# Memory rows transposed before their norm is known, and the first weights asked for earlier, in a hybrid streaming encoder step

## The chip, the cores and the metric

The kernel runs on one core of a Trainium2 chip. Its time is the device time of one execution in microseconds (us). The median of three runs is the number that is compared.

## The reference

One inference step of a one-layer trunk, all in float32: 1024 prompt frames and 8 x 16 sample frames of width 1024, with stick-breaking attention, a Mamba-2 group and forgetting attention side by side, a cross-attention into 256 memory rows, a SwiGLU feed-forward part and a final norm. The part that matters here is the projection of the memory rows to keys and values, which is written out as an output as well:

```python
def rmsnorm(x, g):
    xf = x.astype(jnp.float32)
    y = xf * lax.rsqrt(jnp.mean(xf * xf, axis=-1, keepdims=True) + EPS)
    return (y * g.astype(jnp.float32)).astype(x.dtype)

def mem_kv(mem, g, wk, wv):              # mem (1, 256, 1024), wk and wv (1024, 1024)
    b, m, _ = mem.shape
    mn = rmsnorm(mem, g)
    k = jnp.einsum('bmd,de->bme', mn, wk).reshape(b, m, X_HEADS, X_HEAD_DIM)
    v = jnp.einsum('bmd,de->bme', mn, wv).reshape(b, m, X_HEADS, X_HEAD_DIM)
    return k, v
```

## The kernel before

All dense products are made of three float32r matmuls: each operand is split into a rounded high part and the remainder, and `mm3` adds high x high, high x low and low x high into one PSUM bank. A weight tile is loaded raw, cast on ScalarE (the high part, line 290) and subtracted on GpSimd in pieces of 256 columns (the low part, line 132, in `pool_tt`).

The kernel begins with constants and small loads (lines 138 to 224): the memory rows `xm` (two tiles of 128 x 1024), five vectors of gains and conv_b and the 32 rows of conv_w as rows of one tile `rows`, two raw weight tiles. One transpose of 72 rows turns `rows` into the columns `cols`; `g_mem` is a slice of them.

Then `mem_proj` runs (lines 812 to 836). `norm_T` squares the memory rows on ScalarE, takes the root with `rstd_of` (GpSimd and VectorE), scales the rows on VectorE, and then transposes them block by block on TensorE; the transposed blocks leave PSUM with the gain as a scale, the high part on ScalarE (line 276), the low part on VectorE (line 277). The projection itself is 16 units, each a weight tile of 256 x 512 (two k blocks) against both tiles of memory rows: 12 matmuls of 512 columns. Four units fill a pair of PSUM banks, which ScalarE copies out (line 833) and SyncE stores twice. At unit n the raw tile of unit n + 2 is asked for and split. The raw tiles are of the pool `st`, eight buffers.

After each unit one step of `aux` is emitted: the norm and the transposition of the prompt's rows in three chunks of 384 (`norm_in`, also by `norm_T`), whose squares write into a tile of the same pool `st`. The projections of the prompt, attention and the rest follow.

The program's text gives priority and data dependences; the order in each engine's queue is written by a planner that runs the program on simulated times (`schedule_with_timeline_sim=True`). All loads and stores go through SyncE's queue, in order.

Of the kernel before, what the change touches and what calls it, by code (L numbers as in the profile page):

```python
# [8 lines left out]
F32 = mybir.dt.float32  # L9
F32R = mybir.dt.float32r  # L10
I32 = mybir.dt.int32
AF = mybir.ActivationFunctionType
ALU = mybir.AluOpType
# [4 lines left out]
P = 128  # L18
D = 1024
KT = D // P  # L20
# [37 lines left out]
def f32(x):  # L58
    return x.bitcast(F32)
# [3 lines left out]
def tile_hybrid_step(ctx: ExitStack, tc: tile.TileContext, a: dict):  # L63
    nc = tc.nc
    ACT, DVE, POOL, PE, SP = nc.scalar, nc.vector, nc.gpsimd, nc.tensor, nc.sync
# [6 lines left out]
    mcst = left.enter_context(tc.tile_pool(name="mcst", bufs=1))  # L72
# [13 lines left out]
    def act_t(dt=F32R, home=None):  # L86
        return (home or actp).tile([P, 3072], dt, tag="act", name="act")
# [4 lines left out]
    def st_t(dt=F32R):  # L92
        return stp.tile([P, 1024], dt, tag="st", name="st")

    def ws_t(dt=F32):
        return wsp.tile([P, T], dt, tag="ws", name="ws")

    def xc_t(dt=F32):
        return xcp.tile([P, 1056], dt, tag="xc", name="xc")

    def sg_t(dt=F32):
        return sgp.tile([P, 512], dt, tag="sg", name="sg")
# [4 lines left out]
    def ps_t(pool, tag):  # L107
        return pool.tile([P, 512], F32, tag=tag, name="ps" + tag)
# [7 lines left out]
    def pT():  # L116
        return ps_t(pst, "t")
# [11 lines left out]
    def pool_tt(out, in0, in1, op):  # L129

        for a0, a1 in pieces_of(out.shape[1]):
            POOL.tensor_tensor(out=out[:, a0:a1], in0=in0[:, a0:a1], in1=in1[:, a0:a1], op=op)  # L132

    def small(n, dt=F32):
        return sm.tile([P, 16], dt, tag="sm", name="sm")[:, :n]


    xm = act_t(F32)
    for i in range(2):
        SP.dma_start(out=xm[:, i * D:(i + 1) * D], in_=a["mem_prompt"][0, i * P:(i + 1) * P, :])  # L140
    rows = xc_t()
    for i, g in enumerate(("norm_mix_g", "norm_x_g", "norm_ffn_g", "mem_norm_g", "conv_b")):
        SP.dma_start(out=rows[8 * i:8 * i + 8, :P], in_=a[g][0].rearrange("(k p) -> k p", p=P))
    SP.dma_start(out=rows[40:72, :P], in_=a["conv_w"][0].rearrange("i (k p) -> (i k) p", p=P))
    first_raw = []
    for k0 in (0, 2):
        first_raw.append(st_t(F32))
        SP.dma_start(out=first_raw[-1].rearrange("p (k n) -> p k n", n=512),
                     in_=a["wk_x"][0][k0 * P:(k0 + 2) * P, 0:512].rearrange("(k p) n -> p k n", p=P))


    ident = cst.tile([P, P], F32, name="ident")
# [2 lines left out]
    DVE.tensor_copy(identr, ident)  # L155
    mhalf = cst.tile([P, 1], F32, name="mhalf")
    POOL.memset(mhalf, -0.5)

    mask_sb = mcst.tile([P, P], F32R, name="mask_sb")
    mask_fx = mcst.tile([P, P], F32R, name="mask_fx")  # L160
# [55 lines left out]


    colp = pT()
    PE.transpose(colp[:, :72], rows[:72, :P], ident[:72, :72])
    cols = cst.tile([P, 72], F32, name="cols")  # L220
    DVE.tensor_copy(cols, colp[:, :72])
    DVE.tensor_scalar(cols[:, 32:72], cols[:, 32:72], 0.5, None, ALU.mult)
    g_mix, g_x, g_ffn, g_mem = (cols[:, 8 * i:8 * i + 8] for i in range(4))
    conv_b = cols[:, 32:40]

    hb = mcst.tile([P, 28], F32, name="hb")
    lf = mcst.tile([P, NBLK, 4], F32, name="lf")
    dts = mcst.tile([P, NBLK, 8], F32, name="dts")

# [19 lines left out]
    def rstd_of(ss, n, inv):  # L249
        v, r, t, r2 = small(n), small(n), small(n), small(n)  # L250
        POOL.tensor_scalar(v, ss, inv, EPS, ALU.mult, ALU.add)  # L251
        POOL.tensor_tensor(out=r, in0=v, in1=mhalf.to_broadcast([P, n]), op=ALU.pow)
        DVE.scalar_tensor_tensor(t, r, -0.5, r, ALU.mult, ALU.mult)
        DVE.tensor_tensor(out=t, in0=t, in1=v, op=ALU.mult)
        DVE.scalar_tensor_tensor(r2, t, 1.5, r, ALU.add, ALU.mult)
        return r2

    def norm_T(xs, g, hl, width, inplace=None):


        n = len(xs)
        xn = xs if inplace is not None else [ws_t() for _ in range(n)]
        ss = small(n)
        for i in range(n):
            ACT.activation(inplace if inplace is not None else xn[i][:, :D], xs[i], AF.Square,
                           accum_out=ss[:, i:i + 1])
        r = rstd_of(ss, n, 1.0 / D)
        for i in range(n):
            DVE.tensor_scalar(xn[i][:, :D], xs[i], r[:, i:i + 1], None, ALU.mult)
        yield  # L270
        hi, lo = hl()
        for k in range(KT):
            ps = pT()
            for i in range(n):
                PE.transpose(ps[:, i * P:(i + 1) * P], xn[i][:, k * P:(k + 1) * P], ident)
            ACT.activation(hi[:, k, :], ps[:, :width], AF.Copy, scale=g[:, k:k + 1])
            DVE.scalar_tensor_tensor(lo[:, k, :], ps[:, :width], g[:, k:k + 1], f32(hi[:, k, :]),
                                     ALU.mult, ALU.subtract)
            yield
# [6 lines left out]
    def unit_pair():  # L286
        return [ring.tile([P, 1056], F32R, tag=t, name=t) for t in ("wh", "wl")]

    def split_into(hi, lo, raw, eng=POOL):
        ACT.copy(hi, raw)  # L290
        if eng is POOL:
            pool_tt(lo, raw, f32(hi), ALU.subtract)
        else:
            eng.tensor_tensor(out=lo, in0=raw, in1=f32(hi), op=ALU.subtract)

    def split_unit(raw, n):
        hi, lo = unit_pair()
        split_into(hi[:, :n], lo[:, :n], raw[:, :n])
        return hi, lo

    def raw_t():

        return ring.tile([P, 528], F32, tag="wr", name="wr", bufs=4)

    def w_unit(srcs, k0, nk, raw=None, pair=None, eng=POOL):

        n = sum(s[2] for s in srcs)
        raws = [raw_t(), raw_t()] if raw is None else [raw]
        nk_ = nk // len(raws)
        for i, r in enumerate(raws):  # L310
            rv = r[:, :nk_ * n].rearrange("p (k n) -> p k n", n=n)
            o = 0
            for w, c0, cn in srcs:
                r0 = (k0 + i * nk_) * P
                SP.dma_start(out=rv[:, :, o:o + cn],
                             in_=w[r0:r0 + nk_ * P, c0:c0 + cn].rearrange("(k p) n -> p k n", p=P))
                o += cn
        hi, lo = pair or unit_pair()
        for i, r in enumerate(raws):
            sl = slice(i * nk_ * n, (i + 1) * nk_ * n)  # L320
            split_into(hi[:, sl], lo[:, sl], r[:, :nk_ * n], eng)
        return (hi[:, :nk * n].rearrange("p (k n) -> p k n", n=n),
                lo[:, :nk * n].rearrange("p (k n) -> p k n", n=n))
# [94 lines left out]
    def drain(g):  # L418
        for _ in g:
            pass  # L420
# [391 lines left out]
    def mem_proj(xm, aux):  # L812

        mh, ml = act_pair(256)
        drain(norm_T([xm[:, i * D:(i + 1) * D] for i in range(2)], g_mem, lambda: (mh, ml), 256, xm[:, 2 * D:]))
        work = [(a[wname][0], j, k0, sc, out) for wname, sc, out in (("wk_x", mk_sc, "p_mem_k"), ("wv_x", mv_sc, "p_mem_v"))
                for j in range(2) for k0 in (0, 2, 4, 6)]
        nxt = [[t[:, :1024].rearrange("p (k n) -> p k n", n=512) for t in split_unit(raw, 1024)] for raw in first_raw]
        for n, (w, j, k0, sc, out) in enumerate(work):
            wh, wl = nxt.pop(0)  # L820
            if n + 2 < len(work) :
                w2, j2, k2 = work[n + 2][:3]
                nxt.append(w_unit([(w2, j2 * 512, 512)], k2, 2, st_t(F32)))
            if k0 == 0:
                ps = [(pd, pS)[j % 2]() for _ in range(2)]
            for i in range(2):
                for k in range(2):
                    sl = slice(i * P, (i + 1) * P)
                    mm3(ps[i], mh[:, k0 + k, sl], ml[:, k0 + k, sl], wh[:, k, :], wl[:, k, :],
                        k0 + k == 0, k0 + k == KT - 1)  # L830
                if k0 == 6:
                    t = sg_t()
                    ACT.copy(t, ps[i])
                    for dst in (sc, a[out][0, 0].rearrange("m h d -> m (h d)")):
                        SP.dma_start(out=dst[i * P:(i + 1) * P, j * 512:(j + 1) * 512], in_=t)
            next(aux, None)


# [1065 lines left out]
    for kt in range(2, NFT):  # L1904
        nxt, ahead = left_factors(kt + 1, POOL) if kt + 1 < NFT else iter(()), []
# [57 lines left out]
    for c in range(NCH):  # L1963
# [3 lines left out]
        for f in range(NFT):  # L1967
            raw, hid = raw2_t(), slot()[:, :CW]
# [58 lines left out]
```

## Time and profile before

| | |
|---|---|
| median of three runs | 1915.68 us (1913.57 to 1916.64) |
| the profiled execution's own time | 1915.89 us |
| its span, first to last instruction | 1914.2 us |
| TensorE busy | 1837.6 us, 96% of the span |
| VectorE, ScalarE, GpSimd busy | 897.1, 823.7, 622.6 us |
| granted TensorE clock, mean | 0.988 |

The span is what the trace shows of the execution; 1.7 us lie around it. A busy TensorE is one with a matmul under way, whether at the upper or at the lower level of its clock.

### The profile page before, as it was taken

To read this page: it belongs to the slowest core of one execution; us is meant where nothing else is said; L and a number is where in the kernel's file an instruction comes from. 1 tells how busy PE (TensorE), PEld (TensorE's weight loads), DVE (VectorE), ACT (ScalarE), POOL (GpSimd) and SP (SyncE) were. 2 spreads that over 40 slices of the span, in tenths; PEclk is the share of its full clock that TensorE was granted. 3 is DMA by queue.
4 is the path that set the end of the run, shared out by engine and by line. 5 is a ranking of instruction groups with operands and counts; after the bars stand their busy time and mean duration, and the time that the engine had idled before them with its cause. 6 is when DMAs were issued, how large, how long until landed. Compare 5 with 4: busy or idle time off the path is not lost. (4 is left out here: it accounts for less than half of the span.)

```text
span 1914.2 us, 32508 instructions
## 1 busy us (share of the span) xinstructions
PE 1837.6 (96%) x12146; PEld 1641.4 (86%) x12146; DVE 897.1 (47%) x1823; ACT 823.7 (43%) x1782; POOL 622.6 (33%) x921
## 2 busy tenths in 40 slices
PE   7989989999998889999999999999999999999998
PEld 5889877888876667898998889999999999888886
DVE  3421323457646873353445387333333433455554
ACT  6431534545566771243433275333333333344443
POOL 7532416254324563211102205544444443000000
PEclk9999998999999999999999999999999999999999
DMA  9455645536579887244558124322323223567572
GB/s 336 142 165 159 211 115 152 154 109 185 166 220 282 280 290 260 103 150 145 176 194 291 66 91 111 80 70 70 95 74 75 70 70 100 190 194 237 177 246 92
DMA packets 309742, 305.70 MB, mean 160 GB/s; under 512 B 89996, under 2 KB 261108, under 8 KB 309584
## 3 DMA queue, kind: packets, MB, share of 16 engines
q1 hardware_dynamic: 309584, 303.62, 51.6%
q8 instruction: 96, 1.57, 0.3%
q14 instruction: 62, 0.51, 0.1%
HBM read 229.31 MB, written 74.24 MB: 159 GB/s over the span
## 5 line engine op out<-in xcount | busy, mean ns | idle before, releaser
L132 POOL TENSOR_TENSOR wl<-wr,wh 128x256 fp32r<-128x256 f32 (+2 forms) x184 | 138.6, 787 | 222.4 <-ACT wh L290 202.0
L326 PE MATMUL psd<-act,wh 128*128 128x384 f32 x576 | 198.7, 345 | 5.1 <-DVE sg L453 2.7
L327 PE MATMUL psd<-act,wh 128*128 128x384 f32 x576 | 197.6, 343 | 0.0
L328 PE MATMUL psd<-act,wl 128*128 128x384 f32 x576 | 196.8, 342 | 0.7 <-POOL wl L132 0.7
L1849 PE MATMUL pst<-bT,tr 128*128 128x256 f32 (+1 forms) x1068 | 155.0, 293 | 0.0
L1849 PEld LDWEIGHTS pst<-bT,tr 128*128 128x128 f32 x1068 | 144.9, 188 | 0.1
L328 PE MATMUL psd<-wh,act 128*128 128x512 f32 (+3 forms) x424 | 135.8, 322 | 0.0
L326 PE MATMUL psd<-wh,act 128*128 128x256 f32 (+3 forms) x414 | 133.0, 324 | 2.4 <-ACT pt L1445 1.2
L1849 PE MATMUL psd<-bT,tr 128*128 128x320 f32 (+1 forms) x912 | 133.2, 295 | 0.8 <-DVE tr L1693 0.5
L327 PE MATMUL psd<-wl,act 128*128 128x256 f32 (+3 forms) x414 | 132.8, 322 | 0.5 <-POOL wl L132 0.5
L1849 PEld LDWEIGHTS psd<-bT,tr 128*128 128x128 f32 x912 | 124.7, 188 | 1.8 <-DVE tr L1693 0.7
L326 PEld LDWEIGHTS psd<-act,wh 128*128 128x128 f32 x576 | 109.1, 189 | 8.7 <-DVE sg L453 3.1
L132 POOL TENSOR_TENSOR tr<-u,tr 128x256 fp32r<-128x256 f32 x110 | 81.9, 774 | 102.3 <-ACT tr L1689 85.1
L328 PEld LDWEIGHTS psd<-act,wl 128*128 128x128 f32 x576 | 108.9, 189 | 2.3 <-POOL wl L132 1.0
L327 PEld LDWEIGHTS psd<-act,wh 128*128 128x128 f32 x576 | 109.0, 189 | 1.5 <-issue 1.1
L132 POOL TENSOR_TENSOR ws<-ws 128x256 f32<-128x256 f32 (+2 forms) x100 | 68.5, 713 | 115.3 <-DVE ws L519 99.9
L1824 DVE TENSOR_TENSOR tr<-tr,pst 128x256 f32<-128x256 f32 (+1 forms) x86 | 38.6, 449 | 139.5 <-ACT tr L1821 106.3
L251 POOL TENSOR_SCALAR sm<-sm 128x1 f32<-128x1 f32 (+2 forms) x27 | 7.1, 261 | 296.6 <-ACT y L1932 208.0
L132 POOL TENSOR_TENSOR tr<-raw,tr 128x256 fp32r<-128x256 f32 x94 | 69.2, 765 | 84.5 <-ACT tr L1689 76.3
L1689 ACT CAST tr<-tr 128x384 fp32r<-128x384 f32 (+1 forms) x70 | 37.7, 538 | 121.1 <-DMA tr<-hidsc 104.3
L290 ACT CAST wh<-wr 128x512 fp32r<-128x512 f32 (+2 forms) x90 | 52.2, 621 | 80.7 <-PE psd L328 31.0
L326 PEld LDWEIGHTS psd<-wh,act 128*128 128x128 f32 x414 | 78.3, 189 | 9.9 <-ACT pt L1445 1.5
(620 smaller groups left out, 4714.0 us busy)
## 6 DMA issues: line engine op xcount, KB each, us to landing
u<-w_down SPq DMA_DIRECT2D x40, 512.0 KB
raw<-w_down SPq DMA_DIRECT2D x26, 512.0 KB
st<-qksc SPq DMA_DIRECT2D x48, 256.0 KB
wr<-w_in SPq DMA_DIRECT2D x44, 256.0 KB
tr<-hidsc SPq DMA_DIRECT2D x57, 192.0 KB
hidsc<-tr SPq DMA_DIRECT2D x34, 288.0 KB
qksc<-sg SPq DMA_DIRECT2D x48, 192.0 KB
wr<-cache_sb_k SPq DMA_DIRECT2D x32, 256.0 KB
```

The source lines that it names most:

```text
L132: POOL.tensor_tensor(out=out[:, a0:a1], in0=in0[:, a0:a1], in1=in1[:, a0:a1], op=op)
L251: POOL.tensor_scalar(v, ss, inv, EPS, ALU.mult, ALU.add)
L290: ACT.copy(hi, raw)
L326: PE.matmul(out, ah, bh, start=start, stop=False)
L327: PE.matmul(out, ah, bl, start=False, stop=False)
L328: PE.matmul(out, al, bh, start=False, stop=stop)
L1689: ACT.copy(hi, src)
L1824: DVE.tensor_tensor(out=at(out, g), in0=at(x, g), in1=ps[g][:, :GW[g]], op=op)
L1849: PE.matmul(dst[g][:, :GW[g]], x[:, ka], y[:, k, :], start=start and k == 0 and m == 0, stop=stop and k == 3 and m == 2, skip_group_check= ...
```

## The change

Four edits, all in the first part of the program.

The memory rows are transposed as they were loaded. Their squares and the root (`root`) are emitted after the first unit, and the root is applied to the finished products, as the scale of the copy out of PSUM.

The loads are put in another order: the first memory tile, the five small vectors, the second memory tile, four raw weight tiles instead of two, then conv_w. In `mem_proj` the raw tile is asked for four units ahead and split two units ahead. The low part of units 0, 1, 2, 5, 8, 11 and 14 is subtracted on VectorE in one instruction of 1024 columns, that of the others on GpSimd as before.

conv_w's rows have a transpose of their own (`tap_columns`), emitted after the second unit; the first transpose has 40 rows instead of 72.

A copy of one column on ScalarE stands ahead of all its other work, so that its function table is asked for there.

```diff
-    xm = act_t(F32)
-    for i in range(2):
+    xm, rows = act_t(F32), xc_t()
+    first_raw = []
+
+    def load_xm(i):
         SP.dma_start(out=xm[:, i * D:(i + 1) * D], in_=a["mem_prompt"][0, i * P:(i + 1) * P, :])
-    rows = xc_t()
+
+    def load_wk(n):
+
+        first_raw.append(st_t(F32))
+        SP.dma_start(out=first_raw[-1].rearrange("p (k n) -> p k n", n=512),
+                     in_=a["wk_x"][0][2 * n * P:(2 * n + 2) * P, 0:512].rearrange("(k p) n -> p k n", p=P))
+
+    load_xm(0)
     for i, g in enumerate(("norm_mix_g", "norm_x_g", "norm_ffn_g", "mem_norm_g", "conv_b")):
         SP.dma_start(out=rows[8 * i:8 * i + 8, :P], in_=a[g][0].rearrange("(k p) -> k p", p=P))
-    SP.dma_start(out=rows[40:72, :P], in_=a["conv_w"][0].rearrange("i (k p) -> (i k) p", p=P))
-    first_raw = []
-    for k0 in (0, 2):
-        first_raw.append(st_t(F32))
-        SP.dma_start(out=first_raw[-1].rearrange("p (k n) -> p k n", n=512),
-                     in_=a["wk_x"][0][k0 * P:(k0 + 2) * P, 0:512].rearrange("(k p) n -> p k n", p=P))
+    load_xm(1)
+    for n in range(4):
+        load_wk(n)
+    SP.dma_start(out=rows[64:96, :P], in_=a["conv_w"][0].rearrange("i (k p) -> (i k) p", p=P))
...
+    ACT.activation(small(1), mhalf, AF.Copy, scale=1.0)
...
-    PE.transpose(colp[:, :72], rows[:72, :P], ident[:72, :72])
+    PE.transpose(colp[:, :40], rows[:40, :P], ident[:40, :40])
     cols = cst.tile([P, 72], F32, name="cols")
-    DVE.tensor_copy(cols, colp[:, :72])
-    DVE.tensor_scalar(cols[:, 32:72], cols[:, 32:72], 0.5, None, ALU.mult)
+    DVE.tensor_copy(cols[:, 0:40], colp[:, :40])
+
+    def tap_columns():
+        tp = pT()
+        PE.transpose(tp[:, :32], rows[64:96, :P], ident[64:96, 64:96])
+        DVE.tensor_copy(cols[:, 40:72], tp[:, :32])
+        DVE.tensor_scalar(cols[:, 32:72], cols[:, 32:72], 0.5, None, ALU.mult)
...
-    def split_unit(raw, n):
+    def split_unit(raw, n, eng=POOL):
         hi, lo = unit_pair()
-        split_into(hi[:, :n], lo[:, :n], raw[:, :n])
+        split_into(hi[:, :n], lo[:, :n], raw[:, :n], eng)
         return hi, lo
...
-        drain(norm_T([xm[:, i * D:(i + 1) * D] for i in range(2)], g_mem, lambda: (mh, ml), 256, xm[:, 2 * D:]))
...
-        nxt = [[t[:, :1024].rearrange("p (k n) -> p k n", n=512) for t in split_unit(raw, 1024)] for raw in first_raw]
+
+        def unit(n):
+
+            return [t[:, :1024].rearrange("p (k n) -> p k n", n=512)
+                    for t in split_unit(first_raw.pop(0), 1024, DVE if n < 2 or n % 3 == 2 else POOL)]
+        nxt = [unit(0)]
+
+        for k in range(KT):
+            tp = pT()
+            for i in range(2):
+                PE.transpose(tp[:, i * P:(i + 1) * P], xm[:, i * D + k * P:i * D + (k + 1) * P], ident)
+            ACT.activation(mh[:, k, :], tp[:, :256], AF.Copy, scale=g_mem[:, k:k + 1])
+            DVE.scalar_tensor_tensor(ml[:, k, :], tp[:, :256], g_mem[:, k:k + 1], f32(mh[:, k, :]), ALU.mult, ALU.subtract)
+        nxt.append(unit(1))
+        ss, rstd = small(2), []
+
+        def root():
+            for i in range(2):
+                tc.keep_in_program_order(ACT.activation(xm[:, 2 * D:], xm[:, i * D:(i + 1) * D], AF.Square,
+                                                        accum_out=ss[:, i:i + 1]))
+            r = xm_r[:, 0:2]
+            DVE.tensor_copy(r, rstd_of(ss, 2, 1.0 / D))
+            rstd.append(r)
         for n, (w, j, k0, sc, out) in enumerate(work):
             wh, wl = nxt.pop(0)
-            if n + 2 < len(work) :
-                w2, j2, k2 = work[n + 2][:3]
-                nxt.append(w_unit([(w2, j2 * 512, 512)], k2, 2, st_t(F32)))
+            if n + 4 < len(work):
+                w2, j2, k2 = work[n + 4][:3]
+                first_raw.append(st_t(F32))
+                SP.dma_start(out=first_raw[-1].rearrange("p (k n) -> p k n", n=512),
+                             in_=w2[k2 * P:(k2 + 2) * P, j2 * 512:(j2 + 1) * 512].rearrange("(k p) n -> p k n", p=P))
+            if n + 2 < len(work):
+                nxt.append(unit(n + 2))
...
-                    ACT.copy(t, ps[i])
+                    ACT.activation(t, ps[i], AF.Copy, scale=rstd[0][:, i:i + 1])
...
+            if n == 0:
+                root()
+            if n == 1:
+                tap_columns()
             next(aux, None)
```

## Rows read from the trace of the kernel before

**Rows 1.** The page: busy time, share of the span and instructions, by engine.
```profile
PE 1837.6 (96%) x12146; PEld 1641.4 (86%) x12146; DVE 897.1 (47%) x1823; ACT 823.7 (43%) x1782; POOL 622.6 (33%) x921
```

**Rows 2.** TensorE in order of time: start, duration, instruction, [idle before <-releaser].
```profile
7.03 0.35 PE L219 MATMUL pst<-ident,xc 72*128 72x72 f32 x1 [7.03 <-DMA xc<-conv_w]
9.98 0.90 PE L275 MATMUL pst<-ident,act 128*128 128x128 f32 x3 [2.59 <-DVE act L269]
...
12.16 0.80 PE L326 MATMUL psd<-wh,act 128*128 128x512 f32 x1
12.75 0.63 PE L327 MATMUL psd<-wl,act 128*128 128x512 f32 x1
13.18 0.63 PE L326 MATMUL psd<-wh,act 128*128 128x512 f32 x1
...
16.57 0.39 PE L328 MATMUL psd<-wh,act 128*128 128x512 f32 x1
16.80 0.40 PE L327 MATMUL psd<-wl,act 128*128 128x512 f32 x1
...
23.51 1.14 PE L275 MATMUL pst<-ident,ws 128*128 128x128 f32 x9
25.54 1.60 PE L275 MATMUL pst<-ident,ws 128*128 128x128 f32 x9 [0.89 <-DVE act L277]
...
70.56 0.39 PE L328 MATMUL pss<-wh,act 128*128 128x512 f32 x1
```

**Rows 3.** Stretches: length, then busy time of PE, PEld, DVE, ACT, POOL.
```profile
28.00:48.00 20.00, 20.00 (x89) 15.85 (x90) 2.81 (x5) 14.36 (x22) 19.84 (x30) 1.00 1.07 372
...
130.00:500.00 370.00, 351.43 (x2593) 315.39 (x2592) 157.19 (x272) 167.44 (x390) 149.19 (x219) 0.97 0.54 152
```

**Rows 4.** TensorE from 0 to 75 us, by line: count, busy us, mean ns.
```profile
L275 PE MATMUL pst<-ident,ws 128*128 128x128 f32 x57 | 9.2, 279 | 2.1 <-DVE act L277 1.2 <-DVE ws L269 0.9
```

**Rows 5.** ScalarE in order of time.
```profile
0.78 1.28 ACT L265 ACT_TABLE_LOAD   x1 [0.78 <-PEq L2015]
4.18 1.06 ACT L265 ACTIVATE act<-act 128x1024 f32<-128x1024 f32 x1 [2.11 <-DMA act<-mem_prompt]
...
5.68 1.06 ACT L265 ACTIVATE act<-act 128x1024 f32<-128x1024 f32 x1 [0.35 <-DMA act<-mem_prompt]
...
11.63 1.20 ACT L276 ACTIVATE act<-pst,cols 128x256 fp32r<-128x256 f32 x3 [0.73 <-PE pst L275]
...
25.66 1.05 ACT L290 CAST wh<-st 128x1024 fp32r<-128x1024 f32 x1
```

**Rows 6.** SyncE's queue in order of time: start, duration, transfer.
```profile
0.79 0.87 SPq L140 DMA_DIRECT2D act<-mem_prompt  x2
1.71 0.37 SPq L143 DMA_DIRECT2D xc<-norm_mix_g  x1
...
4.17 1.82 SPq L148 DMA_DIRECT2D st<-wk_x  x2
...
6.55 1.54 SPq L437 DMA_DIRECT2D ws<-x_prompt  x3
...
11.20 4.13 SPq L437 DMA_DIRECT2D ws<-x_prompt  x4
...
16.14 4.18 SPq L315 DMA_DIRECT2D st<-wk_x  x5
```

**Rows 7.** GpSimd from 26 to 71 us, by line.
```profile
L132 POOL TENSOR_TENSOR wl<-st,wh 128x256 fp32r<-128x256 f32 x52 | 39.1, 789 | 7.8 <-ACT wh L290 7.7
```

**Rows 8.** VectorE over the whole span, by line and shape.
```profile
L1697 DVE TENSOR_TENSOR u<-u 128x640 f32<-128x640 f32 x8 | 6.6, 822 | 0.0
```

**Rows 9.** VectorE in order of time, alone and beside GpSimd.
```profile
8.16 0.16 DVE L254 TENSOR_TENSOR sm<-sm 128x2 f32<-128x2 f32 x1
...
48.29 0.65 DVE L254 TENSOR_TENSOR sm<-sm 128x3 f32<-128x3 f32 x1
```

**Rows 10.** What TensorE waited for, whole span: us in total, times, longest.
```profile
PE pst L888 <- DMA wr<-cache_sb_k: 5.8, 4, 4.9
```

More of the change, by code (lines that the diff above doesn't have):

```diff
@@ L226, in tile_hybrid_step @@
     hb = mcst.tile([P, 28], F32, name="hb")
+    xm_r = mcst.tile([P, 2], F32, name="xm_r")
     lf = mcst.tile([P, NBLK, 4], F32, name="lf")
```

## The prediction

> **What bounds the kernel now.** I read the page first, for who is busy: TensorE is at work for 96% of the span [rows 1], so time is won only where TensorE idles, where it runs at the lower of its two clock levels, or where it does less. The change touches one stretch, the memory projection at the start, so everything after that was read by stages and by waits, and the start in order of time.
>
> The start in order of time [rows 2]: TensorE does nothing until 7.03 us, and then one small transpose that waited for conv_w. The memory rows' transposes begin at 9.98 us, after VectorE has scaled the rows by the root. The first projection matmul starts at 12.16 us. From 12.75 to 13.18 us is 0.43 us for 512 columns, which is the lower level (1.2 GHz); 16.57 to 16.80 us is 0.23 us, the upper (2.4 GHz). The last projection matmul starts at 70.56 us, so the projection ends at about 70.8. Between 28 and 48 us TensorE is busy throughout, and GpSimd nearly so [rows 3]: there they are balanced. So what can be won lies ahead of 12.16 us and in the holes; the largest hole is around 25.54 us.
>
> The count of work: 16 units of 12 matmuls, 192 x 0.232 = 44.5 us at the upper level. Woven in are 57 transposes of the prompt's normalised rows [rows 4] at 1.14/9 = 0.127 us [rows 2], 7.2 us, and 16 of the memory rows, 2.0 us. With two matmuls of the next projection (0.4) that is 54.1 us. From 9.98 to 70.8 us are 60.8 us, so 6.7 us go to holes and to the lower level.
>
> **The change, part by part.**
>
> *Unscaled transposes.* Removed from the path before the first matmul: two squares, the root's GpSimd and VectorE operations, and two scalings. What remains before it is the memory rows, the gain column, a cast and a product. Landing: the first memory tile is issued at 0.79 us and its square starts on landing at 4.18 us, 3.4 us later; the next tile's square starts at 5.68 us, 1.5 us for 512 KB [rows 5, 6]. After: first tile 0.79 to 1.22, five gain loads of at most 0.37 us, second tile at about 3.1, first weight tile at 3.5 us (4.17 before). With 3.4 us the second memory tile lands at 6.5 us, and the weights between 6.9 (latency alone) and 8.0 us (1.5 us behind the memory tile); I take 7.6, nearer the queue. The gains land by 6.5 us, and no longer wait for conv_w. So the transposes begin at about 6.5 instead of 9.98, ScalarE's evacuations (0.40 us each, three in 1.20) at about 7.2, the weight cast (1.05 us) ends at 8.7, and the first matmul starts at 8.9 us: 3.3 us earlier. Bounds: 2.5 us (weights at 8.0, one evacuation ahead of the cast), 4.0 us.
>
> *Clock.* TensorE reached the upper level some 6 us after its transposes began [rows 2]. After the change its work is sparse from 6.5 and dense from 8.9 us, so I put the rise at 14 us: 5 us at half rate lose 2.5 us, with bounds 1.6 and 3.
>
> *The root on products.* The squares (1.06 us each) move behind unit 2's cast on ScalarE, the root's operations behind them. The first product that needs the root ends with unit 3, about 20 us, and the root is due by about 15 us: nothing on the path. The scale on the evacuation adds no instruction. What is queued behind the squares on ScalarE is unit 3's cast and the prompt's squares; ScalarE is busy 14.4 of 20 us in the stretch beyond [rows 3], which covers it. Were that cover gone, unit 3's cast would come 2.1 us late.
>
> *Subtractions on VectorE.* Units 0, 1, 2, 5, 8, 11, 14 go from GpSimd to VectorE, 7 of 16. GpSimd does 4 pieces of 0.79 us a unit, 3.1 us [rows 7], beside 2.8 us of TensorE. VectorE's nearest row is 640 elements in 0.82 us [rows 8]; by size 1024 are 1.31 us, and between 0.82 and two of them, 1.64. In three units GpSimd then needs 6.3 us, TensorE 8.4 and more with transposes. For units 0 and 1 it saves some 1.8 us each just where TensorE starts. Two engines on SBUF disturb each other: a VectorE operation on two or three columns took 0.16 us alone and 0.65 us beside GpSimd [rows 9]. So five of the moved subtractions may wait up to a GpSimd piece, 0.79 us; 0 to 4 us on VectorE, which has room. I take 0 for the path. The Trainium skill (SBUF — State Buffer, Who interferes with whom) says that VectorE with two SBUF inputs and GpSimd lock a port pair for a whole instruction and the other blocks. By that, GpSimd and VectorE add up, 6.3 + 1.3 = 7.6 us in three units; that is still under TensorE's 8.4, and the trace's 0.16 against 0.65 us agrees with the rule.
>
> *Four units ahead.* Before, units 3 to 7 were issued from 16.14 us only, behind seven prompt tiles [rows 6], and unit 3's cast ran at 25.66 us [rows 5]: this is the hole at 25.54 us. TensorE used part of it for the prompt's transposes. After, units 0 to 3 are issued ahead of every prompt tile, 1.5 us apart, landing by 12.5 us, and unit 4 stands right behind. TensorE needs unit 5 at about 8.9 + 60 x 0.232 + 2.5 + 24 x 0.127 = 28.4 us. If unit 5 comes no earlier than unit 3 did (25.7), cast and subtraction end at 28.1. So the hole closes, but barely; 1.2 us are kept for this and the smaller holes (bounds 0 and 4).
>
> *Table.* The only load at the start runs at 0.78 us, 1.28 us long, and ScalarE then idles until 4.18 us [rows 5]: asked early it saves 0. The Trainium skill (ScalarE: Activation LUTs, What ACT_TABLE_LOAD costs) gives some 2.66 us for a switch of sets. By that, if the copy drew another set than the square, a second load would fall before the squares, and the sum would be up to that much later; no row here shows a second load beside these two functions.
>
> *conv_w's columns.* One more 32-row transpose, copy and halving, some 0.8 us over three engines, beside other work; taken as 0, with 0.4 us of TensorE (the row at 7.03 us) as the bound.
>
> **The sum.** First matmul 8.9, work 44.5 + 7.2 + 0.4, half of the memory transposes still inside (1.0), lower level 2.5, holes 1.2: the projection ends at 65.7 us, against 70.8. That is 5.1 us, taken as 5.0. TensorE bounds what follows, so the shift carries to the end. The profiled execution is 1915.89 us (span 1914.2), 0.2 above the median of 1915.68; the same gain off the median gives 1910.7 us. With every bound on its good side the gain is 5.0 + 0.7 + 0.9 + 1.2 = 7.8 us, with every bound on its bad side 5.0 - 0.8 - 0.5 - 2.8 = 0.9 us, so this case's own range is 1908 to 1915; most of it lies below 1912, since all bad sides together are rare.
>
> **Rivals.** About 0.2% (3.8 us) is what a measurement of this kernel tells from no change: below 1911.9 is faster, above 1919.5 slower.
>
> *The hole only moves.* Units 5 and on are still issued behind prompt tiles; the buffer that the prompt's squares use is asked for between units 4 and 5 from the same pool, and unit 3 had stood behind it in the same way. For it: the order of the SP queue [rows 6]. Against it: two more units in hand, 5.6 us of TensorE. Price: the hole of 2.8 us around 25.54 us stays, so the gain is 5.0 - 2.8 = 2.2 us: 1913.5 us.
>
> *Given back later.* The queues' order is written by a planner on simulated times, so a start 5 us earlier also reorders what follows. TensorE waits 5.8 us in four places for cache_sb_k tiles, 4.9 of them at once [rows 10]; a load planned behind one more store there costs as much again: 5.0 - 4.9, 1915.6 us. Against it: most of the order follows data and program order.
>
> *Slower.* The same mechanism at full price: between 130 and 500 us TensorE idles 18.6 of 370 us [rows 3]. If the new order raises that by half, 9.3 us, the result is 1915.7 - 5.0 + 9.3 = 1920.0 us. It decides from 8.8 us of added idle time on. For it: this stretch mixes five engines' work with loads and holds the longest waits; against it: nothing in the change touches it.
>
> **How the numbers follow.** Forecast 0.56, hole moves 0.18, given back 0.13, slower 0.13. Faster: 0.50 of the forecast's 0.56 and 0.02 of the moved hole, 0.52. Slower 0.13, the rest 0.35. The predicted time is the likeliest case, 1910.7 us. The range reaches down to 1905.5 (all holes and a kinder order later) and up to 1918.5, which takes in the moved hole and the given-back case and leaves out most of the slower one.
>
> **What would show it.** Right: the first projection matmul near 8.9 us, its last ending near 66; no wait of TensorE over 1 us between 10 and 66 us; VectorE rows of 1024 elements at 1.2 to 1.7 us; the same four table loads; stages after the projection as long as before. Wrong: a wait for a cast around 22 to 30 us (moved hole); idle time between 130 and 500 us clearly over 18.6 us (given back, slower); a first matmul after 10 us, which would fell the landing times.

## Result, and the profile after

The changed kernel took 1921.43 us (median of 9 runs, 1916.33 to 1924.77), the kernel before 1916.15 us beside it (9 runs). The ratio is 1.0029, 95% interval 1.0016 to 1.0042: slower by 0.3%, where 1910.7 us were forecast. Run again later it gave 1921.98 us, ratio 1.0017 (1.0001 to 1.0033). Its profiled execution took 1924.77 us, the slowest of the nine, so single differences of this trace are checked below against other traces.

The page of the changed kernel, engines [rows 1]: GpSimd works 17 us less, VectorE 5 us more, TensorE is busy 13 us longer with one instruction more.

```profile
PE 1850.5 (96%) x12147; PEld 1651.2 (86%) x12147; DVE 902.3 (47%) x1830; ACT 825.0 (43%) x1783; POOL 605.7 (31%) x893
```

TensorE in order of time in the changed kernel [rows 2]:

```profile
5.38 0.30 PE L228 MATMUL pst<-ident,xc 40*128 40x40 f32 x1 [5.38 <-DMA xc<-conv_b]
5.61 1.72 PE L842 MATMUL pst<-ident,act 128*128 128x128 f32 x6
...
9.18 1.22 PE L341 MATMUL psd<-wh,act 128*128 128x512 f32 x2
...
13.17 0.57 PE L343 MATMUL psd<-wh,act 128*128 128x512 f32 x1
13.58 0.39 PE L341 MATMUL psd<-wh,act 128*128 128x512 f32 x1
...
26.30 1.14 PE L290 MATMUL pst<-ident,ws 128*128 128x128 f32 x9
28.55 1.60 PE L290 MATMUL pst<-ident,ws 128*128 128x128 f32 x9 [1.11 <-DVE act L292]
30.42 1.43 PE L290 MATMUL pst<-ident,ws 128*128 128x128 f32 x6 [0.28 <-DVE act L292]
31.75 1.22 PE L341 MATMUL pss<-wh,act 128*128 128x512 f32 x2
33.01 0.80 PE L342 MATMUL pss<-wl,act 128*128 128x512 f32 x1
33.61 0.59 PE L343 MATMUL pss<-wh,act 128*128 128x512 f32 x1
34.03 0.40 PE L341 MATMUL pss<-wh,act 128*128 128x512 f32 x1
...
66.14 0.40 PE L343 MATMUL pss<-wh,act 128*128 128x512 f32 x1
66.38 1.03 PE L290 MATMUL pst<-ident,ws 128*128 128x128 f32 x8
```

The first projection matmul starts at 9.18 us, the upper clock level is there at 13.58, and the last projection matmul ends at 66.4. But from 26.3 to 31.75 us TensorE has no projection work: it runs 24 of the prompt's transposes with holes of 1.11 and 0.28 us between them, and the projection resumes at the lower level (33.01 to 33.61). Eight more transposes come behind the projection's end.

SyncE's queue says why [rows 6]:

```profile
3.37 2.16 SPq L147 DMA_DIRECT2D st<-wk_x  x4
...
6.10 0.44 SPq L860 DMA_DIRECT2D st<-wk_x  x1
6.58 2.05 SPq L452 DMA_DIRECT2D ws<-x_prompt  x3
...
15.39 4.18 SPq L452 DMA_DIRECT2D ws<-x_prompt  x4
19.61 2.78 SPq L330 DMA_DIRECT2D wr<-w_in  x4
22.43 3.27 SPq L860 DMA_DIRECT2D st<-wk_x  x3
25.80 3.09 SPq L860 DMA_DIRECT2D st<-wv_x  x5
```

Units 0 to 4 are asked for by 6.5 us, units 5 to 7 only from 22.43 us, behind seven prompt tiles and four tiles of the next projection: the hole of the kernel before, two units further on.

The two stretches [rows 3], columns as there (the last three: granted clock, DMA share, GB/s). From 28 to 48 us GpSimd is no longer full, but the clock is at 0.91; from 130 to 500 us TensorE idles 21.4 us, before 18.6.

```profile
28.00:48.00 20.00, 19.13 (x79) 14.39 (x80) 10.56 (x15) 15.95 (x25) 13.78 (x18) 0.91 1.05 380
130.00:500.00 370.00, 348.62 (x2549) 313.62 (x2547) 153.29 (x258) 162.29 (x378) 146.38 (x216) 0.96 0.53 152
```

VectorE's subtractions over the first 66 us, by line and shape (count, busy us, mean ns), and ScalarE's start [rows 5]:

```profile
L309 DVE TENSOR_TENSOR wl<-st,wh 128x1024 fp32r<-128x1024 f32 x7 | 10.2, 1455 | 5.1 <-ACT wh L305 5.1
```

```profile
0.78 1.28 ACT L166 ACT_TABLE_LOAD   x1 [0.78 <-PEq L2059]
2.08 0.20 ACT L166 ACTIVATE sm<-mhalf 128x1 f32<-128x1 f32 x1
6.93 1.21 ACT L843 ACTIVATE act<-pst,cols 128x256 fp32r<-128x256 f32 x3 [4.65 <-PE pst L842]
```

What TensorE waited for, whole span [rows 10]: the wait for cache_sb_k is as before. The wait for L771, small VectorE copies, takes 3.9 us at two places; the kernel before waits 1.0 us at one for the same copies (its L756).

```profile
PE pst L932 <- DMA wr<-cache_sb_k: 5.8, 3, 4.9
...
PE psd L775 <- DVE so L771: 3.9, 2, 3.0
```

**Where the time went.** Matmuls of the same line and tiles were paired between two traces, and their shift was read at fixed points of the first trace of the kernel before (median of the pairs starting within 3 us before to 6 us behind a point). A stretch's length is its length there plus the change of the shift. The shift at 8 us is taken as zero, so the first column holds all that a kernel has won or lost since its beginning. Another choice of pairs moves single lengths by up to 2 us. "Idle" and "lower level" are what TensorE stood and what it ran at the lower clock level in 312 to 412. Labels of experiments are explained below; the later order is the one in which the planner put the instructions between 290 and 450 us, where the two kernels differ; behind about 450 us it is the same but for one swap of two neighbours. The three kernels with the copies moved are an exception: their order differs between 500 and 600 us too, by more than a hundred matmuls. Lengths are in us.

| kernel | later order | 8-72 | 72-222 | 292-455 | 312-412 | idle | lower level |
|---|---|---|---|---|---|---|---|
| before | before | 64.0 | 150.0 | 163.0 | 100.0 | 2.8 | 0.0 |
| before_again | before | 65.3 | 150.5 | 165.2 | 101.3 | 2.7 | 3.4 |
| root_at_1 | before | 62.0 | 151.4 | 163.7 | 101.1 | 3.5 | 0.0 |
| tap_at_9 | before | 63.1 | 152.1 | 162.7 | 102.5 | 3.5 | 3.6 |
| pad_24 | before | 57.3 | 155.7 | 162.0 | 101.8 | 2.7 | 3.4 |
| after | after | 60.5 | 153.4 | 169.5 | 105.3 | 5.7 | 8.4 |
| after_again | after | 63.2 | 151.6 | 168.5 | 105.3 | 5.7 | 8.5 |
| tap_at_6 | after | 60.4 | 152.1 | 169.3 | 105.2 | 5.8 | 8.2 |
| subtract_only | after | 60.7 | 152.7 | 166.9 | 103.9 | 5.9 | 3.5 |
| tails_first | after | 60.7 | 152.6 | 165.9 | 104.2 | 5.8 | 3.7 |
| before_scratch | after | 62.4 | 150.0 | 168.2 | 104.0 | 5.8 | 3.4 |
| hole_fixed | after | 56.1 | 154.2 | 166.0 | 104.2 | 5.7 | 3.4 |
| both_fixed | after | 54.5 | 152.5 | 168.3 | 105.2 | 5.7 | 8.2 |
| pad_20 | after | 55.7 | 152.9 | 167.9 | 104.9 | 6.4 | 3.6 |
| tails_own | after, copies moved | 62.7 | 154.0 | 164.9 | 101.2 | 2.9 | 1.5 |
| tails_own_scratch | after, copies moved | 55.6 | 153.9 | 158.4 | 101.2 | 2.9 | 0.0 |
| before_tails_own | before, copies moved | 65.0 | 154.3 | 159.0 | 99.4 | 2.2 | 0.0 |

Means of the two traces of each kernel, after minus before: 61.9 - 64.7 = -2.8 us at the start, 152.5 - 150.3 = +2.2 from 72 to 222, 169.0 - 164.1 = +4.9 from 292 to 455. The start won less than forecast, most of it was gone by 222 us, and the loss came 230 us behind the last changed line. With another choice of pairs the 4.9 us lie between 4.6 and 6.3.

**Idle time or clock, over the whole span.** The two traces of each kernel, before and before_again, after and after_again, with their mean granted clock:

```profile
core 0: 1914.2 us, clock 0.988
core 0: 1917.7 us, clock 0.988
core 0: 1923.1 us, clock 0.985
core 0: 1926.5 us, clock 0.984
```

The span is 8.9 and 8.8 us longer, but TensorE does not idle longer: span less busy time is 76.6 and 78.7 us before, 72.6 and 78.1 after. What grew is the time at the lower clock level, in the clock records of the traces: 46.7 and 46.5 us before, 61.5 and 63.1 after. TensorE was at work in 34.1 and 35.1 of it before, in 50.3 and 46.6 after; at half speed the 16.2 and 11.5 us more cost some 8.1 and 5.8 us (an estimate from these numbers). Both traces of the changed kernel are the slowest execution of their series, so the whole is smaller in the median. The 12 executions of after_again have a mean clock of 0.9874, the 29 of the kernel before beside them 0.9890; 0.0016 of 1922 us are at most 3.1 us, of the 3.9 us between the two medians. Only a part of the added time at the lower level can be tied to a wait below.

### The profile page after: what moved, and what is told of

It is laid out like the page before. It is cut to its first block, busy times and chain, and to the rows that moved or that the text cites. A ratio compares the mean times of both kernels' runs of the same rounds, so it can differ in the third digit from the quotient of the medians.

```text
span 1923.1 us, 32481 instructions
## 1 busy us (share of the span) xinstructions
PE 1850.5 (96%) x12147; PEld 1651.2 (86%) x12147; DVE 902.3 (47%) x1830; ACT 825.0 (43%) x1783; POOL 605.7 (31%) x893
## 5 line engine op out<-in xcount | busy, mean ns | idle before, releaser
L1733 ACT CAST tr<-tr 128x384 fp32r<-128x384 f32 (+1 forms) x70 | 37.7, 538 | 122.5 <-DMA tr<-hidsc 104.8
```

What stands on the lines that cost most here:

```text
L1733: ACT.copy(hi, src)
```

## The experiments

Every run stands beside runs of the kernel before on the same chip; the ratio is to those. The theory at the start was that the gain of the start is real but small for the hole, and the planner's other order between 290 and 450 us costs more. The rivals were that the hole and the clock at 26 to 35 us are the whole loss, or that one wait makes the other order dear.

**The later order, by edits that should cost nothing.** The change with the tap columns made later, or the root later; and the kernel before with only the subtractions moved.

```
-            if n == 1:
+            if n == 6:          # tap_at_6; n == 9 in tap_at_9
                 tap_columns()
-            if n == 0:
+            if n == 1:          # root_at_1
                 root()
```

```
 # subtract_only: the kernel before, units 0, 1, 2, 5, 8, 11, 14
-    def split_unit(raw, n):
+    def split_unit(raw, n, eng=POOL):
...
-        split_into(hi[:, :n], lo[:, :n], raw[:, :n])
+        split_into(hi[:, :n], lo[:, :n], raw[:, :n], eng)
```

> The change whole, conv_w's columns emitted after unit 6 instead of unit 1. The planned order of the work after the memory projection is that of the changed kernel. Theory (the later order costs the time): as slow as the changed kernel, about 1.003 times the kernel before, the loss lying between 290 and 450 us. Rival (the new start itself costs it, through the hole at 26 us and its drop of the clock): the same, 1.003.

> The change whole, conv_w's columns emitted after unit 9 instead of unit 1. The planned order after the memory projection is that of the kernel before. Theory (later order): the 8 us between 290 and 450 us are gone and the 3 us won at the start stay, 0.998 times the kernel before, some 1912 us. Rival (new start): nothing gained by it, 1.003.

> The kernel before with one part of the change alone: units 0, 1, 2, 5, 8, 11 and 14 subtracted on VectorE. Its planned order after the memory projection is that of the changed kernel. Theory (later order): slower than before by the 8 us of 290 to 450 us less up to 2 us won in the holes of the projection, 1.003 to 1.004. Rival (new start): the start is the old one, so 0.999 to 1.000.

> The change whole, the root emitted after unit 1 instead of unit 0. The planned order after the memory projection is that of the kernel before. Theory (later order): 0.998 times the kernel before, as with conv_w's columns after unit 9. Rival (new start): 1.003.

Measured: tap_at_6 1925.09 us, ratio 1.0039 (1.0025 to 1.0052); tap_at_9 1919.40, 1.0012 (0.9999 to 1.0025); subtract_only 1920.09, 1.0009 (1.0001 to 1.0018); root_at_1 1918.37, 1.0005 (0.9992 to 1.0018). tap_at_6 and tap_at_9 hold the same change and differ by one small transpose's place; the first has the changed kernel's later order, the second that of before, and they are 5.7 us apart. subtract_only, which keeps the old start, comes out with the new order too. In the table, 292 to 455 us takes 163.3 us on average in the five traces with the order of before and 167.8 in the nine with that of after: 4.5 us. But tap_at_9 and root_at_1 aren't faster than the kernel before, where the theory had 0.998, so the start's gain isn't in the total either. subtract_only missed both of its forecasts, 1.003 to 1.004 and 0.999 to 1.000.

**One wait inside that order.** Around 403 us, TensorE in the changed kernel:

```profile
398.18 0.33 PE L341 MATMUL psd<-act,wh 128*128 128x384 f32 x1
398.35 0.34 PE L342 MATMUL psd<-act,wh 128*128 128x384 f32 x1
...
400.21 0.23 PE L577 MATMUL pss<-mask_sb,identr 128*128 128x128 f32 x1
403.47 0.39 PE L775 MATMUL psd<-ident,so 128*27 128x128 f32 x1 [3.03 <-DVE so L771]
403.79 0.69 PE L341 MATMUL psd<-act,wh 128*128 128x384 f32 x1
404.27 0.52 PE L342 MATMUL psd<-act,wh 128*128 128x384 f32 x1
404.59 0.52 PE L343 MATMUL psd<-act,wl 128*128 128x384 f32 x1
```

VectorE there:

```profile
400.48 1.74 DVE L786 SCALAR_TENSOR_TENSOR xc<-xc,cols 128x1024 f32<-128x1024 f32 x1
402.14 0.49 DVE L787 SCALAR_TENSOR_TENSOR sg<-sg,cols 128x128 f32<-128x128 f32 x1
402.56 0.69 DVE L770 COPY so<-xc 128x3 f32<-128x3 f32 x1
403.16 0.16 DVE L771 COPY so<-sg 128x24 f32<-128x24 f32 x1
```

L775 transposes the last columns of a convolution. The copies that fetch them, 3 and 24 columns, stand behind the whole chain of taps; TensorE waits 3.03 us, and its next matmuls are 0.32 us apart, before the wait 0.17: the lower clock level. All nine kernels traced with this order have the wait, 3.0 to 3.1 us. In the kernel before (trace of before_again) the copies stand ahead of the chain:

```profile
415.92 0.17 DVE L755 COPY so<-xc 128x3 f32<-128x3 f32 x1 [3.44 <-ACT xc L751]
415.99 0.81 DVE L768 TENSOR_SCALAR xc<-xc,cols 128x1024 f32<-128x1024 f32 x1
416.72 0.17 DVE L756 COPY so<-sg 128x24 f32<-128x24 f32 x1
...
417.06 1.28 DVE L771 SCALAR_TENSOR_TENSOR xc<-xc,cols 128x1024 f32<-128x1024 f32 x1
```

Two edits were tried on this, with and without a cure of the hole: the prompt's first squares write their unread result into a tile of the pool xc, no longer into st. Two more kernels hold that cure and idle transposes, at whose count the planner falls into the one order or the other.

```
 # tails_first
+            with tc.high_priority(200):
                 DVE.tensor_copy(tails[:, 0:3], ...)
                 DVE.tensor_copy(tails[:, 3:27] ...)
 # both_fixed, pad_20, pad_24, hole_fixed
-        return norm_T(xs, g_mix, hl, CW, st_t(F32))
+        return norm_T(xs, g_mix, hl, CW, xc_t()[:, :D] if c == 0 else st_t(F32))
 # pad_20 (5 turns), pad_24 (6), in mem_proj
+            if n == 14:
+                for _ in range(5):
+                    tp = pT()
+                    for i in range(4):
+                        PE.transpose(tp[:, i * P:(i + 1) * P], ident, ident)
```

> The changed kernel, with the two tiny VectorE copies of the convolution's last columns (L770, L771: 3 and 24 columns) given a high priority, so that they stand ahead of the tap chain in VectorE's queue; every other engine's order stays the changed kernel's later order. Theory 1, one wait: the later order costs its time at one place, where TensorE stands 3.0 us for those copies at 400 us and then runs 6.8 us at half its clock, 3.0 + 6.8/2 = 6.4 us; both go, and the time is 1921.4 - 6.4 = 1915.0, with some of it met again behind: 1915 to 1918.5, ratio 0.999 to 1.001. Theory 2, the later order costs in many small places: under 2 us come back, ratio 1.002 to 1.003. Theory 3, the loss is the slow stretch and the hole at 26 to 35 us: nothing comes back, ratio 1.003.

> As tails_first, and the prompt's first squares take their scratch from the pool xc, so that loads of units 5 to 7 no longer stand behind the prompt tiles. Theory 1: the tails' 6.4 us as in tails_first, and beside it the hole (1.4 us idle of TensorE, 3.4 us at half clock, 1.7) are gone: 3 us under tails_first, 1912 to 1915, ratio 0.997 to 0.999, a kernel that beats both. Theory 3: this one, and not tails_first, falls under the changed kernel by 3 us. If leads at the start are lost again at the loads that come due at 86 us, it equals tails_first within 1 us.

> The changed kernel with the same scratch from xc, and 20 transposes of the identity (about 0.13 us each, 2.6 us, results unread) after unit 14; the planner's later order stays the changed kernel's. Theory 1: the 3 us wait at L775 and the slow stretch at 400 us are there; 1919.5 to 1922, ratio 1.001 to 1.003. Theory 3: the hole is gone, and with it the loss: ratio under 1.001.

> pad_20 with 24 transposes in place of 20, 0.5 us more work, at which the planner comes out with the later order of the kernel before. Theory 1: no 3 us wait at L775 and no slow stretch at 400 us, so 4 to 7 us below pad_20 in spite of the four transposes more: 1914 to 1917, ratio 0.998 to 1.000. Theory 3, and any that leaves the later order out: 0.5 us above pad_20.

Measured: tails_first 1923.01 us, 1.0032 (1.0017 to 1.0046); both_fixed 1918.93, 0.9995 (0.9977 to 1.0014); pad_20 1920.34, 1.0009 (0.9993 to 1.0025); pad_24 1918.18, 1.0001 (0.9983 to 1.0019). tails_first missed its aim: the first pair of copies didn't move, and the wait is there, 3.0 us. So it says nothing on theory 1. From tails_first to both_fixed, which adds the hole's cure, the medians fall by 4.1 us and the ratios by 0.37%, more than the 3 us expected. pad_24 is 2.2 us below pad_20 with four transposes more, and has no wait at L775; the direction is theory 1's and the intervals overlap.

**The copies without the buffer.** Their target was a ring of four buffers (so); the convolution's own tile has unused columns.

```
-            tails = sg2_t()
+            tails = xs_[:, 160:416]
```

> The changed kernel with the convolution's last columns copied into unused columns of the tile they come from, and no longer into a buffer of the ring so (four buffers), for which they stood behind the tap chain whatever their priority. The later order stays the changed kernel's but for the rows around these copies. Theory 1, one wait: the 3.0 us at L775 go, and with them the slow stretch at 400 us (3.4 to 6.8 us at half clock, 1.7 to 3.4 us): 4.7 to 6.4 us under the changed kernel run beside it, ratio to the kernel before 0.9990 to 1.0005. Theory 2, many small places: under 2 us of it come back, ratio 1.002 to 1.003.

> tails_own, and the scratch of the prompt's first squares from xc as in both_fixed, so that the hole at 26 us is gone. Theory 1: as tails_own, less up to 3 us (both_fixed, with the wait at 400 us still there, was at 0.9995): 0.9965 to 0.9985, better than both kernels. Theory 2: equal to both_fixed, 0.999 to 1.000.

> The kernel before with the same copies into the tile they come from: the control. There the copies stood ahead of the chain and nobody waited over 1 us for them. Both theories: the time of the kernel before within 1.5 us, ratio 0.999 to 1.001. If it is faster by more, a gain of tails_own is not the wait's.

> The changed kernel itself, beside the three on one chip, for a second trace and a direct difference. Expected 1.002 to 1.004. If the slow stretch at 31 us, the 3 us wait at L775 and the slow stretch at 403 us belong to the program they are there again; if they belonged to the one execution they are not.

Measured: tails_own 1916.48 us, 0.9990 (0.9976 to 1.0004); tails_own_scratch 1911.61, 0.9955 (0.9938 to 0.9973); before_tails_own 1911.95, 0.9975 (0.9957 to 0.9993); after_again 1921.98, 1.0017 (1.0001 to 1.0033). What TensorE waited for from 280 to 460 us in tails_own has no line of L775 any more:

```profile
PE pst L932 <- DMA wr<-cache_sb_k: 5.5, 3, 5.0
PE pst L969 <- POOL ws L132: 2.5, 2, 1.8
PE pss L917 <- ACT kf L934: 2.4, 2, 1.2
```

By the trace theory 1 holds in its place: 312 to 412 us takes 101.2 us and idles 2.9, as in the order of before. But the control fell: the kernel before gains 0.25% by the same edit without that wait, as much as the changed kernel's 0.27% (0.9990 against 1.0017). From 292 to 455 us it gains 5.1 us (164.1 to 159.0), the changed kernel 4.1 (169.0 to 164.9). The edit also moves the planner's order between 500 and 600 us, so it isn't a test of the wait alone. So the time that the edit won can't be booked on the wait, and how much of the total the wait is stays open. after_again repeats the wait and the slow stretches at 32 and 404 us, so these are no chance of the first trace; tails_first, with the same hole, has no slow stretch at 32 us. Here the projection itself waited too:

```profile
29.72 1.07 PE L290 MATMUL pst<-ident,ws 128*128 128x128 f32 x6 [0.27 <-DVE act L292]
32.87 1.22 PE L341 MATMUL pss<-wh,act 128*128 128x512 f32 x2 [2.08 <-ACT wh L305]
```

**What the hole cost, and what cures it.** The forecast missed by more than the parts found so far, so four more runs: the kernel before itself, the cure alone on either kernel, and the cure with all subtractions on GpSimd.

```
 # hole_fixed_pool: hole_fixed, and
-split_unit(first_raw.pop(0), 1024, DVE if n < 2 or n % 3 == 2 else POOL)
+split_unit(first_raw.pop(0), 1024, POOL)
```

> The kernel before itself, for a second trace. Expected 0.9995 to 1.0005. If the lead is given back between 72 and 222 us, this stretch takes 150 us again; if the first trace was a quick execution, 152 to 154 us, as in the 13 other traces (151.4 to 155.7). The stretch from 292 to 455 us should take 162 to 164 us, as in all kernels with its later order.

> The changed kernel with the scratch of the prompt's first squares from xc, nothing else; the later order is the changed kernel's. If the hole is what eats the start: 8 to 72 us take 54.5 to 56 us (60.4 to 63.2 with the hole), no slow stretch at 31 us, and 5 to 7 us under the changed kernel, ratio 0.999 to 1.000. If the hole is worth only its idle time and the slow stretch after it (3 us): 58 us and 1.0010 to 1.0020.

> The kernel before with the same scratch from xc, nothing of the change; its later order comes out as the changed kernel's. If the change's earlier loads, unscaled rows and VectorE subtractions are worth the 5 us that were forecast once the hole is gone: 8 to 72 us take 59 to 61 us here against 55 in hole_fixed, ratio 1.0020 to 1.0030. If the scratch alone gives all: 55 to 56 us, and the time of hole_fixed.

> hole_fixed with all sixteen subtractions on GpSimd. If VectorE's part matters: GpSimd, which took 19.8 of 20 us from 28 to 48 us in the kernel before, bounds the projection again, 8 to 72 us take 59 to 61 us, ratio 1.0015 to 1.0025. If not: as hole_fixed within 1 us.

Measured: before_again 1918.85 us, 1.0002 (0.9990 to 1.0015); hole_fixed 1916.88, 1.0000 (0.9983 to 1.0017); before_scratch 1918.91, 1.0002 (0.9992 to 1.0012); hole_fixed_pool 1916.91, 0.9995 (0.9984 to 1.0006). With the cure the queue asks for units 5 to 7 at 10.24 us, as the trace of hole_fixed shows:

```profile
6.78 0.46 SPq L860 DMA_DIRECT2D st<-wk_x  x1
7.28 1.92 SPq L452 DMA_DIRECT2D ws<-x_prompt  x3
10.24 3.63 SPq L860 DMA_DIRECT2D st<-wk_x  x3
```

and TensorE is busy and at the upper level throughout, in a stretch where the changed kernel stood at 0.96 and 0.92 in its two traces (columns as in the stretches above):

```profile
30.00:72.00 42.00, 42.00 (x223) 35.82 (x222) 25.51 (x35) 31.75 (x52) 32.19 (x41) 1.00 0.82 271
```

The start takes 54.5 to 56.1 us in the three traces with the change and the cure alone or with the tails' edits, 60.4 to 63.2 in the five of the change with the hole, 62.4 in before_scratch. So the hole cost some 6 us of the start, and without it the change is worth 6.3 us against the same kernel without the change. In time, though, hole_fixed and before_scratch are 2.0 us apart with intervals that overlap; what reaches the end of those 6.3 us (from one trace each) wasn't settled. The subtractions on VectorE weren't needed: with all on GpSimd the last projection matmul starts at 63.75 us against 61.99 in hole_fixed, and the time is the same. before_again again takes 150.5 us from 72 to 222, and 165.2 from 292 to 455 where 162 to 164 were expected. Most kernels that come early take 151.4 to 155.7 from 72 to 222, so the lead is given back there in the main. That the lead is the reason isn't shown: before_scratch came 1.6 us early and took 150.0, before_tails_own took 154.3 without any lead. One wait goes with the length in many of the traces, that for tiles loaded from qksc, an intermediate result in HBM. From 72 to 222 us in the kernel before and in hole_fixed:

```profile
PE pss L560 <- DMA st<-qksc: 0.3, 1, 0.3
PE pss L575 <- DMA st<-qksc: 2.9, 2, 2.2
```

It is 1.0 us in before_again and before_scratch, 2.0 in before_tails_own, 2.1 to 2.6 in pad_20, tails_own and tails_own_scratch; but pad_24 took 155.7 us without it. No run tested it.

## Why the prediction was wrong

*The step that failed* is the last one, "TensorE bounds what follows, so the shift carries to the end". TensorE is 96% busy, yet of the start's gain (2.8 us in the mean of two traces) about 2.2 were gone by 222 us, and the planner's other order took 4.9 us between 292 and 455. The step also took a busy TensorE for one at the upper level: the sum prices the lower level at the start alone, and the changed kernel's traces spent 15 to 17 us more at it over the whole span, without idling longer. Both losses lie in "given back later" and "slower", which together had 0.26, but not by the mechanism that "given back" names: the wait for cache_sb_k is 5.8 us before and after. Why the lead went and why the lower level came more often stays open.

*First matmul* 9.18 us for 8.9, *clock* up at 13.58 for 14 us: right. The lower level came back at 31 us, which the sum didn't hold: 3.4 us there, 1.7 lost, and 6.8 us in after_again.

*Four units ahead* was mis-sized in its main condition. Unit 5 was needed at 26.3 us, not 28.4, and ran at 31.75 us (32.87 in the other trace); the "hole only moves" rival, with the mechanism as written there, is what happened. Its price was 2.8 us and measured about 6 in that start (1.6 to 3.6 us of idle time, 1.7 to 3.4 us by the clock where it fell, and transposes that were pushed behind the projection; how these add up to the 6 us isn't settled).

*The projection's end* at 66.4 us met the forecast of 65.7, in the other trace 69.1. It wasn't the right mark: eight of the prompt's transposes had slipped behind it, and the matmuls that follow were only 0.8 to 3.5 us early.

*Table, conv_w's columns, root on products:* nothing on the path, as forecast, though the root was there at 19.9 us and not by 15; the first product that needs it ended at 23.7. One table load at 0.78 us, four in the whole span as before, each 1.28 us. *Subtractions on VectorE:* 1.46 us each for the 1.31 estimated, GpSimd relieved (13.78 of 20 us for 19.84); that they cost the path nothing fits hole_fixed and hole_fixed_pool, whose times are equal.

*The slower rival* had the place and the sign, not the price: idle time from 130 to 500 us rose by 2.8 us, not 9.3, and its point of decision, 8.8 us of added idle time, wasn't reached. Three parts are in the result: a start gain cut by the hole, a lead given back, and 4.9 us from 292 to 455 us, in which one wait of 3.0 us and the lower clock level behind it are the part that the traces show. What each is worth in the median isn't shown.

## What to carry to other kernels

A gain at the start of a planned program has to be followed to the end on the same matmuls: compare the order of all queues first, because the place of one small transpose at the start set the order of queues 300 us later, and the two versions lie 5.7 us apart. Compare the time at the lower clock level too: in the two traces of the changed kernel it grew, and TensorE's idle time did not. When loads are pulled ahead, look at what else takes buffers from their pool: a scratch tile that nobody reads held back three loads and cost some 6 us of the start. Look also at tiny copies that a long chain overtakes; here they came in front once their target was no longer a buffer of the ring. The two small cures together with the change gave 1911.61 us, ratio 0.9955, the best kernel here. But the kernel before with the copies' cure alone took 1911.95 us beside it, with intervals that overlap, so of that gain the change's own part isn't shown.

## What the runs showed of the hardware

After a wait TensorE may run on at the lower level although its work is dense again: behind the 3.03 us at 403 us the granted clock was at half for 6.8 us, 3.4 us lost on top of 3.0. In five other traces of the same order that stretch was 3.4 us, with the same wait. The order of before has a smaller wait there: 1.96 us in before_again, with 3.4 us at the lower level behind it; 1.26 and 0.71 us in the first trace of the kernel before, with none.

The tap chain is slow where GpSimd works beside it: a tap of 1024 columns took 1.74 us at 400 us in the changed kernel, with GpSimd in its subtractions, and 1.28 us at 417 us in before_again, where GpSimd had nothing to do. That made the copies later still. The Trainium skill (SBUF — State Buffer, Who interferes with whom) says that a VectorE instruction with two SBUF inputs contends with a GpSimd instruction that reads SBUF; these rows agree.

One program's runs spread by 10 us and more: the kernel before took 1908.4 to 1925.7 us over 29 runs of one job. The clock goes with it: in the four series of the kernel before, a mean granted clock lower by 0.001 went with 0.8 to 1.2 us more, and over the 18 traces the shortest span (1906.0 us) has 37.7 us at the lower level, the longest (1926.5) 63.1. A difference of two traces is no measure of two programs at this size; the table needed 17.
